# Hybrid decoder block on one core: two of the four mixer sums are split straight from their tiles, and block four splits its key, value and gate weights from the raw matrix

## The chip, the cores and the metric

The kernel runs on one NeuronCore of a Trainium2 chip. Five engines work side by side and meet through semaphores: PE (TensorE, matmuls, with PEld for the weight loads that overlap them), DVE (VectorE), ACT (ScalarE), POOL (GpSimd) and SP (SyncE, which issues most DMAs here). The metric is device time in microseconds (us) of one execution, as a median over several runs.

## The reference, cut to what matters

One layer of a hybrid decoder on 2048 tokens of width 1024, all in float32. The parts that the change touches are the combined projection and what makes its right-hand sides:

```
h = RMSNorm_pre(x) * (1 + scale) + shift
one combined projection h W_in -> [attn q|k|v, mLSTM q|k|v|o, mLSTM i|f pre-gates, branch gates A|B]
branch A: causal sliding-window (128) GQA, rotary on q/k, learned per-head sinks, banded blocks
branch B: causal depthwise conv4 + SiLU on mLSTM q/k, chunkwise-parallel stabilised mLSTM,
          per-head layer norm, sigmoid output gate
merged = sigmoid(g_A) * (y_A W_A) + sigmoid(g_B) * (y_B W_B); mix = merged W_out
x = x + gate * RMSNorm_post(mix); same sandwich + adaLN for the SwiGLU FFN.
```

Attention has 8 query heads and 2 key/value heads of 64; the mLSTM has 4 heads of 128 and chunks of 64. The FFN is 2816 wide.

## The kernel before

**Arithmetic.** Float32 products are made from a rounded high part (`hi`, fp32r) and the remainder (`lo`). mm3 (L212) issues three matmuls for each product: hi by hi, hi by lo, lo by hi. So every operand must first be split: ACT casts it (`A.copy` to fp32r), DVE subtracts the cast from the original. Where an operand is used again, both parts are kept in DRAM ("kept weights") and loaded as pairs, which saves the split.

**Tiling.** The 2048 tokens are four blocks of 512 (b = 0 to 3), called block one to block four here; a superblock sb has two blocks, b0 = 2 sb and b1 = 2 sb + 1. Around the change PE projects, in order, the mLSTM's values for b0 (`vm`), then for b1 key, value and gate pre-activations (`kv`, 264 columns), the query (`q`, 512 columns) and `vm`, with attention and mLSTM steps woven in. A `token_group` takes the weights in pieces of two or four 128-row slabs and accumulates into four PSUM tiles, one for each 128 tokens; when the last piece is done it evacuates the four tiles with ACT (L870 in `vm`, L840 in `kv`), each into a `tx` buffer, from where a DMA stores them. PSUM has four such accumulators, so the next product needs them evacuated.

**The sums.** For the large products after that (the mLSTM's output gate, q and k, and the branch gates, for a whole superblock: `in_pair`) the kernel uses a Strassen-Winograd scheme over the two blocks of a superblock. Its right-hand sides are sums T1 to T4 of h tiles, each 128 x 2048 (1 MB); they stand as plain float32 in tiles of the pool `big` (dictionary HR, written by DVE at L558 to L561). `hsums` splits them into `hi` and `lo` tiles, also of the pool `big`, entered in the dictionary HC by `hc_part(name, i)`. It is called twice for each superblock: for T2 and T4 between `vm` of b0 and `kv` of b1 (L1382), and for T1 and T3 after the rest of `vm` of b1 (L1394). Before, each call copies both sums with a DMA from SBUF to SBUF into the `lo` tile (L569), yields for L_HD (5000), and then makes eight casts (L575) and eight subtractions (L576) of 128 x 512 in place, with a yield of L_HS (1500) after each.

**The weights.** `Raw` tiles hold raw weights (pool `raw`, two buffers), `split` (L267 ACT, L268 DVE) makes the parts (four buffers of each part), `piece` makes the two into a `Part`. For key, value and gates, `load_kv` takes 256 columns of w_in as rows of 1 KB (L819) and 8 columns as rows of 32 bytes (L820). Block one and block two read these raw weights and split them; block two stores the parts in W_D["kv"] (L374, eight stores of 264 KB, because `store` is "kv" when b is not 0). Block three and block four load the parts from there: two loads of 1056 KB each, each into a raw tile (L333), and no split. The query's weights of blocks three and four come as kept parts too: every second piece goes into a raw tile (L333), the others into a pair of split tiles (L328, two loads of 512 KB).

**What sets the order.** Generators yield small steps; a list of pending streams (`spawn`, `tick`, `finish`) is woven with the matmuls by a clock of estimated ns (the L_ numbers), and the Tile scheduler then fixes each engine's list of instructions and its semaphores. Once fixed, each engine works through its own list in order: an ACT cast that waits for a DMA holds up each evacuation behind it, and a DMA on SP's list whose data isn't ready holds up the loads behind it. In these lists every DMA of SP takes one of eight semaphores in turn (DMAHW0 to 7).

**Names in rows.** acc and mix are PSUM tiles; big are the 1 MB tiles of h, of T1 to T4 and their parts; hl is a split pair of `in_pair`'s weights; whi and wlo are parts of weights; at_d, at carry attention operands through DRAM; tm, sp, mx belong to the mixers; vm_d and vmt are the DRAM and SBUF side of `vm`'s result.

Of the kernel before, what the change touches and what calls it, by code (L numbers as in the profile page):

```python
# [10 lines left out]
F32 = mybir.dt.float32  # L11
# [4 lines left out]
ALU = mybir.AluOpType  # L16
# [12 lines left out]
T2 = 1024  # L29
# [9 lines left out]
L_X, L_HT, L_HS = 16000.0, 1400.0, 1500.0  # L39
# [34 lines left out]
def decoder_block(ctx: ExitStack, tc: tile.TileContext, a: dict, out: bass.AP, dbg=None):  # L74
    nc = tc.nc
# [18 lines left out]
    V, A, T, Q = (InOrder(e) for e in (nc.vector, nc.scalar, nc.tensor, nc.sync))  # L94
# [35 lines left out]
    def big(shape, dtype=F32):  # L130
        t = bpool.tile([P, 2048], dtype, tag="big", name=nm("big"))
        return t.rearrange("p (k c) -> p k c", k=shape[0])
# [86 lines left out]
    def spawn(gen, delay=0.0):  # L219
        st = [now[0] + delay, gen, False]  # L220
        streams.append(st)
        return st
# [15 lines left out]
    def finish(sts):  # L238
        for st in sts:
            while not st[2]:  # L240
                now[0] = max(now[0], min(q[0] for q in streams))
                tick()
# [75 lines left out]
    def kept_weights(name):  # L318

        n = 528 if name == "kv" else 1024  # L320
        for j0 in range(0, 4, 2):
            for j in ((j0,) if name == "kv" else (j0, j0 + 1)):
                def load(j=j):
                    src = W_D[name]
                    if name != "kv" and j % 2:
                        parts = [split_tile(x) for x in ("whi", "wlo")]
                        for i in range(2):
                            nc.sync.dma_start(parts[i].bitcast(F32), src[:, j, i, :])  # L328
                        return [parts]
                    m = 2 if name == "kv" else 1  # L330
                    t = wpool.tile([P, RAWC], F32R, tag="raw", name=nm("raw"))
                    v = t[:, :m * 2 * n].rearrange("p (m i c) -> p m i c", m=m, i=2)
                    nc.sync.dma_start(v.bitcast(F32), src[:, j:j + m, :, :])  # L333
                    return [[v[:, q, i, :] for i in range(2)] for q in range(m)]
                raw = Raw(load)
                for q in range(2 if name == "kv" else 1):
                    yield raw, q, 2 * (j + q), 2
# [41 lines left out]
    def srcs_rows(w, nk, c0):  # L379
        for k0 in range(0, nk, 4):  # L380
            kn = min(4, nk - k0)
            raw = raw_rows(w, k0, kn, c0)
            for j in range(0, kn, 2):
                yield raw, (lambda t, j=j: t[:, j:j + 2, :]), k0 + j, 2
# [110 lines left out]
    HC, HR = {}, {}  # L495

    def hc_part(name, i):
        st = HC.setdefault(name, [None, None])
        if st[i] is None:
            st[i] = big([4, TB], F32R)  # L500
        return st[i]
# [59 lines left out]
            V.tensor_tensor(t4, t4, t2, op=ALU.subtract)  # L561
            yield L_HT

    def hsums(names):

        for name in names:
            raw = HR.pop(name)
            lo = hc_part(name, 1)
            nc.sync.dma_start(lo.bitcast(F32), raw)  # L569
        yield L_HD  # L570
        for name in names:
            hi, lo = (hc_part(name, i) for i in range(2))
            for k in range(4):
                v = lo[:, k, :].bitcast(F32)
                A.copy(hi[:, k, :], v)  # L575
                V.tensor_tensor(lo[:, k, :], v, hi[:, k, :].bitcast(F32), op=ALU.subtract)  # L576
                yield L_HS

    def norm_out(xy, t, dst_n, sx):

# [188 lines left out]
    def superblock(sb):  # L769
# [3 lines left out]
        def lhs_h(b):  # L773
            def lhs(kk, t):
                return tuple(p_[:, kk % 4, t * P:(t + 1) * P] for p_ in HC[f"{kk // 4 + 1}{b % 2 + 1}"])
            return lhs
# [33 lines left out]
        def evac_q(b):  # L810
            def evac(t, ps):
                raw = tx([P, 512])
                A.copy(raw, ps)
                R["qk"].append(spawn(q_stream(b, t, rope(raw, HQ, b, t))))
            return evac
# [19 lines left out]
        def evac_kv(b):  # L835
            before = [v_last]

            def evac(t, ps):
                raw = ld([1, 512])[:, 0, :] if b == 0 else tx([P, 392])
                A.copy(raw[:, :264], ps[:, :264])  # L840
                v, dv = raw[:, 128:256], raw[:, 264:392]
                n = b * NT + t
                y = rope(raw, HKV, b, t)
                for i in range(2):
                    A.copy(gt[:, t, 32 * i:32 * i + 4], raw[:, 256 + 4 * i:260 + 4 * i])
                V.tensor_tensor(dv, v, before[0], op=ALU.subtract)
                before[0] = v
                if t == NT - 1:
                    A.copy(v_last, v)
                    before[0] = v_last  # L850
                G.dma_start(at_d[n][:, AT_V + P:], dv)
                if n + 1 < S // P:
                    G.dma_start(at_d[n + 1][:, AT_V:AT_V + P], v)
                R["qk"].append(spawn(k_stream(n, y)))
            return evac

        def q_kv(b):
            if b > 1:
                q = token_group(kept_weights("q"), KD, 512, lhs_h(b), evac_q(b), kept=True)
            else:  # L860
                q = token_group(srcs_rows(w_in, KD, C_Q), KD, 512, lhs_h(b), evac_q(b), pair_heads=True, store="q" if b else None)
            if b > 1:
                return q, token_group(kept_weights("kv"), KD, 264, lhs_h(b), evac_kv(b), kept=True)
            raw_kv = Raw(load_kv)
            return q, token_group([(raw_kv, (lambda r, j=j: r[:, j:j + 2, :]), j, 2) for j in range(0, KD, 2)], KD, 264, lhs_h(b), evac_kv(b), store="kv" if b else None)
# [194 lines left out]
        def attend(b):  # L1060
            finish(R["qk"])
            ready[0] = (b - b0 + 1) * NT
            if b == b0:
                R["att"] = [spawn(attention_stream(0), L_QK), spawn(attention_stream(1), L_QK + L_ATT2)]
            R["gs", b] = [spawn(gates(b), L_QK)]
# [313 lines left out]
        yield lambda: finish([hps[b1]])  # L1379
        if sb == 0:  # L1380
            yield lambda: attend(b0)
        yield lambda: hps.update(t=spawn(hsums(("T2", "T4"))))  # L1382
        q1, kv1 = (list(z) for z in q_kv(b1))
        yield from kv1
        yield from q1
# [5 lines left out]
        def start_f():  # L1391
            finish([hps["t"]])
            HC.pop("12")
            hps["t"] = spawn(hsums(("T1", "T3")))  # L1394

        yield start_f
        pairs = [("om", 0), ("qk", 0), ("om", 1), ("qk", 1), ("ga", 0), ("qk", 2), ("ga", 1), ("qk", 3),
# [22 lines left out]
    hps = {}  # L1420
# [780 lines left out]
    def program():  # L2201
        items = [it for sb in range(NSB) for it in superblock(sb)]
        last = max(i for i, it in enumerate(items) if isinstance(it, Part))
        first_block()
        yield from items[:last]
        yield lambda: next(phase2)
        yield from items[last:]
# [47 lines left out]
```

## Time and profile before

| what | before |
|---|---|
| median of 3 runs | 2662.91 us (2662.21 to 2664.54) |
| profiled execution | 2668.66 us, its span 2667.0 us |
| mean granted clock of PE in it | 0.994 |
| bytes moved by DMA | 532.97 MB, mean 200 GB/s |
| SBUF to SBUF copies of L569 | 8, of 1024 KB each |
| stores of L374 (kv, q, vm parts) | 24 |

One execution is profiled; it is 5.75 us above the median of the runs. The span runs from the first to the last instruction, and 1.66 us of that execution lie around it. In a timeline's row stand the start (us in the span), the duration, the engine, the line, the operation, out<-in, the shape, the count, and in brackets the idle time before it with what ended it. "PEclk" is the share of full clock that PE was granted. A DMA's row on SPq is its issue; "DMA to landing" is the time from there until the data is in place.

### The profile page before, as it was taken

To read this page: it belongs to the slowest core of one execution; us is meant where nothing else is said; L and a number is where in the kernel's file an instruction comes from. 1 tells how busy PE (TensorE), PEld (TensorE's weight loads), DVE (VectorE), ACT (ScalarE), POOL (GpSimd) and SP (SyncE) were. 2 spreads that over 40 slices of the span, in tenths; PEclk is the share of its full clock that TensorE was granted. 3 is DMA by queue.
4 is the path that set the end of the run, shared out by engine and by line. 5 is a ranking of instruction groups with operands and counts; after the bars stand their busy time and mean duration, and the time that the engine had idled before them with its cause. 6 is when DMAs were issued, how large, how long until landed. Compare 5 with 4: busy or idle time off the path is not lost.

```text
span 2667.0 us, 36229 instructions
## 1 busy us (share of the span) xinstructions
PE 2615.5 (98%) x12546; PEld 2145.8 (80%) x12546; DVE 1937.2 (73%) x3758; ACT 1281.9 (48%) x2531; POOL 300.3 (11%) x473
## 2 busy tenths in 40 slices
PE   8999999999989999999999999999999999999998
PEld 6877788888876788888878888888778888888876
DVE  5878887768676988875777777775776767676466
ACT  6656544545654654454643433345554333333444
POOL 0320001101132000210001111110000011001000
PEclk9899999999999999999999999999999999999999
DMA  7785465887787545597765554446675323234556
GB/s 270 255 303 164 135 196 183 291 301 253 262 313 244 166 135 181 183 296 268 220 238 193 184 169 153 163 139 228 213 242 173 111 99 116 90 111 139 199 196 220
DMA packets 327032, 532.97 MB, mean 200 GB/s; under 512 B 23136, under 2 KB 197724, under 8 KB 320064
## 3 DMA queue, kind: packets, MB, share of 16 engines
q1 hardware_dynamic: 287752, 448.45, 50.4%
q0 software_dynamic: 20880, 66.41, 6.6%
q10 hardware_dynamic: 18216, 15.79, 1.9%
q8 instruction: 99, 1.62, 0.2%
q14 instruction: 85, 0.70, 0.1%
HBM read 367.61 MB, written 154.57 MB: 196 GB/s over the span
## 4 chain that ended last, share of the span: by engine, by line
PE 88%; DVE 4%; DMA 3%; ACT 2%; issue 1%; POOL 0%; ACTq 0%; SPq 0%; DVEq 0%; POOLq 0%
PE acc L212 62%; PE mix L212 22%; PE mix L217 2%; PE acc L90 1%; DVE hl L1745 1%; PE mix L90 1%; DMA raw<-as_d 1%; ACT hl L1744 1%; DMA big<-big 0%; DMA raw<-ws_d 0%; DMA raw<-in_w_in_dram 0%; ACT tm L1002 0%; DMA at_d<-tx 0%; DMA raw<-in_w_ffn_down_dram 0%; ACT big L575 0%
## 5 line engine op out<-in xcount | busy, mean ns | idle before, releaser
L212 PE MATMUL acc<-big,hl 128*128 128x512 f32 x3936 | 936.4, 393 | 7.0 <-ACT tx L870 5.4
L212 PEld LDWEIGHTS acc<-big,hl 128*128 128x128 f32 x3936 | 733.8, 188 | 166.4 <-ACT tx L870 5.9
L1744 ACT CAST hl<-raw 128x512 fp32r<-128x512 f32 x732 | 439.9, 621 | 489.6 <-PE acc L212 208.7
L1745 DVE TENSOR_TENSOR hl<-raw,hl 128x512 fp32r<-128x512 f32 x732 | 495.1, 692 | 198.4 <-ACT hl L1744 196.0
L212 PE MATMUL acc<-whi,big 128*128 128x512 f32 (+1 forms) x896 | 281.6, 390 | 3.0 <-ACT tx L870 3.0
L212 PE MATMUL mix<-big,hl 128*128 128x512 f32 x1056 | 263.0, 390 | 1.8 <-ACT hl L1744 1.1
L212 PE MATMUL acc<-hl,hl 128*128 128x512 f32 x1008 | 237.2, 393 | 6.2 <-DVE hl L1745 3.3
L212 PEld LDWEIGHTS mix<-big,hl 128*128 128x128 f32 x1056 | 197.8, 188 | 44.5 <-ACT hl L1744 2.0
L212 PEld LDWEIGHTS acc<-hl,hl 128*128 128x128 f32 x1008 | 187.1, 188 | 51.8 <-DVE hl L1745 8.8
L212 PEld LDWEIGHTS acc<-whi,big 128*128 128x128 f32 x896 | 168.6, 192 | 36.2 <-ACT tx L870 3.4
L212 PE MATMUL mix<-hl,hl 128*128 128x512 f32 x792 | 182.7, 391 | 3.4 <-ACT hl L1744 2.6
L212 PEld LDWEIGHTS mix<-hl,hl 128*128 128x128 f32 x792 | 147.8, 188 | 37.6 <-ACT hl L1744 4.2
L212 PE MATMUL acc<-wlo,big 128*128 128x512 f32 (+1 forms) x448 | 174.4, 389 | 0.0
L212 PE MATMUL acc<-big,whi 128*128 128x512 f32 x512 | 157.3, 393 | 0.0
L268 DVE TENSOR_TENSOR wlo<-raw,whi 128x1024 fp32r<-128x1024 f32 (+1 forms) x76 | 90.8, 1194 | 65.7 <-ACT whi L267 60.2
L267 ACT CAST whi<-raw 128x1024 fp32r<-128x1024 f32 (+1 forms) x76 | 78.4, 1032 | 109.7 <-PE acc L212 103.5
L492 POOL TENSOR_TENSOR rs<-ms,halves 128x1 f32<-128x1 f32 (+1 forms) x56 | 41.3, 744 | 797.8 <-DVE ms L490 750.4
L212 PE MATMUL mix<-hcT4h,hl 128*128 128x512 f32 x352 | 115.6, 389 | 0.7 <-ACT hl L1744 0.7
L212 PE MATMUL acc<-hcT2h,hl 128*128 128x512 f32 x352 | 115.5, 389 | 0.0
L212 PEld LDWEIGHTS acc<-big,whi 128*128 128x128 f32 x512 | 95.3, 188 | 19.3
L212 PEld LDWEIGHTS acc<-wlo,big 128*128 128x128 f32 x448 | 85.8, 192 | 18.0 <-issue 1.2
L212 PE MATMUL acc<-big,wlo 128*128 128x512 f32 x256 | 97.6, 392 | 0.0
(388 smaller groups left out, 3802.3 us busy)
## 6 DMA issues: line engine op xcount, KB each, us to landing
as_d<-w POOLq DMA_DIRECT2D x154, 256.0 KB, 2.5
raw<-in_w_in_dram SPq DMA_DIRECT2D x36, 1024.0 KB, 5.4
raw<-as_d SPq DMA_DIRECT2D x70, 512.0 KB, 3.8
raw<-in_w_ffn_gate_dram SPq DMA_DIRECT2D x22, 1024.0 KB, 6.1
raw<-in_w_ffn_up_dram SPq DMA_DIRECT2D x22, 1024.0 KB, 5.8
raw<-ws_d SPq DMA_DIRECT2D x40, 512.0 KB, 4.6
tx<-in_w_ada_dram SPq DMA_DIRECT2D x64, 256.0 KB, 5.3
g_d<-tx SPq DMA_DIRECT2D x64, 256.0 KB, 2.4
```

What stands on the lines that cost most here:

```text
L90: self.last = tc.keep_in_program_order(f(*p, **k)).ins
L212: T.matmul(o, lhsT=lhsT, rhs=rhs, start=start, stop=stop, skip_group_check=resumed)
L217: T.transpose(o, i, ident[:k, :k])
L267: A.copy(hv, src)
L268: V.tensor_tensor(lv, src, hv.bitcast(F32), op=ALU.subtract)
L492: G.tensor_tensor(r[:, :n], ms[:, :n], nhalf[:, :n], op=ALU.pow)
L1744: A.copy(v(hi), src)
L1745: V.tensor_tensor(v(lo), src, v(hi).bitcast(F32), op=ALU.subtract)
```

## The change

Two edits, and one that follows from the first.

1. `hsums(name, moved)` splits its first sum (T2, then T1) straight from its own tile into new `hi` and `lo` tiles, in four steps with a yield of L_HS after each, with no copy and no wait. Only then the sum's tile is given back, the second sum (T4, then T3) is copied by DMA into its `lo` tile as before, and after L_HD it is split in place as before. Of eight copies four are left.
2. In `q_kv` the kept parts of key, value and gates are read by block three alone (b == 2). Block four goes the way of block two: one raw load of 1 MB and 32 KB from w_in, four splits, and, since `store` is "kv" there too, eight stores of the parts into W_D["kv"], which nobody reads afterwards. The two loads of 1056 KB are gone.

In the changed kernel the lines stand three lower behind hsums (the evacuation of `vm` is L873, the kept loads stay at L333, the store at L374), the direct split is L568 and L569, the copy L573, the split in place L578 and L579, `load_kv` L822 and L823.

```diff
-    def hsums(names):
-
-        for name in names:
-            raw = HR.pop(name)
-            lo = hc_part(name, 1)
-            nc.sync.dma_start(lo.bitcast(F32), raw)
+    def hsums(name, moved):
+
+        hi, lo = (hc_part(name, i) for i in range(2))
+        for k in range(4):
+            A.copy(hi[:, k, :], HR[name][:, k, :])
+            V.tensor_tensor(lo[:, k, :], HR[name][:, k, :], hi[:, k, :].bitcast(F32), op=ALU.subtract)
+            yield L_HS
+        HR.pop(name)
+        lo = hc_part(moved, 1)
+        nc.sync.dma_start(lo.bitcast(F32), HR.pop(moved))
         yield L_HD
-        for name in names:
-            hi, lo = (hc_part(name, i) for i in range(2))
-            for k in range(4):
-                v = lo[:, k, :].bitcast(F32)
-                A.copy(hi[:, k, :], v)
-                V.tensor_tensor(lo[:, k, :], v, hi[:, k, :].bitcast(F32), op=ALU.subtract)
-                yield L_HS
+        hi = hc_part(moved, 0)
+        for k in range(4):
+            v = lo[:, k, :].bitcast(F32)
+            A.copy(hi[:, k, :], v)
+            V.tensor_tensor(lo[:, k, :], v, hi[:, k, :].bitcast(F32), op=ALU.subtract)
+            yield L_HS
...
-            if b > 1:
+            if b == 2:
                 return q, token_group(kept_weights("kv"), KD, 264, lhs_h(b), evac_kv(b), kept=True)
...
-        yield lambda: hps.update(t=spawn(hsums(("T2", "T4"))))
+        yield lambda: hps.update(t=spawn(hsums("T2", "T4")))
...
-            hps["t"] = spawn(hsums(("T1", "T3")))
+            hps["t"] = spawn(hsums("T1", "T3"))
```

How the lists move. First ACT at place 1, T2/T4 of the first superblock, while `vm` of block one ends: whi139 and whi145 are the first two parts of block two's key/value weights, tx141 to tx144 the four evacuations of `vm`, big171 and big206 the high parts of T2 and T4 before. Before:

```order
L267 CAST whi139_1092<-raw121_935 128x528
L575 CAST big171_1252<-big151_1147 128x512 x4
L870 COPY tx141_1104<-acc122_938 128x512
L870 COPY tx142_1113<-acc123_939 128x512
L267 CAST whi145_1134<-raw121_935 128x528
L829 CAST tx114_912<-mix131_989 128x128
L803 ACTIVATE tx126_945<-mix134_1015 128x512
L803 ACTIVATE tx127_950<-mix135_1024 128x512
L575 CAST big206_1495<-big152_1149 128x512 x4
L870 COPY tx143_1122<-acc124_940 128x512
L870 COPY tx144_1131<-acc125_941 128x512
```

and after, with big151 and big200 the high parts of T2 and T4:

```order
L568 CAST big151_1147<-big64_543 128x512
L267 CAST whi139_1092<-raw121_935 128x528
L873 COPY tx141_1104<-acc122_938 128x512
L873 COPY tx142_1113<-acc123_939 128x512
L267 CAST whi145_1134<-raw121_935 128x528
L873 COPY tx143_1122<-acc124_940 128x512
L832 CAST tx114_912<-mix131_989 128x128
L873 COPY tx144_1131<-acc125_941 128x512
L806 ACTIVATE tx126_945<-mix134_1015 128x512
L806 ACTIVATE tx127_950<-mix135_1024 128x512
L578 CAST big200_1448<-big184_1340 128x512 x4
L267 CAST whi159_1195<-raw121_935 128x528
```

T2's casts now lie further up (the last of the four is the first row), all four evacuations stand ahead of T4's casts, and T4's casts ahead of whi159, the third part of the key/value weights.

Next SP at place 3, T2/T4 of the second superblock and block four's key and value. big1323 and big1324 are the lo tiles of T2 and T4, raw1239 and raw1265 the two raw tiles, at1223 an attention operand, vm_d2 the stores of block three's evacuations. Before:

```order
L476 DMA tx1264_7713<-in_w_ada_dram 128x512
L569 DMA big1323_8010<-big1141_6927 128x2048
L954 DMA at1223_7481<-at_d8_198 128x1792
L569 DMA big1324_8012<-big1067_6529 128x2048
L333 DMA raw1239_7547<-w_kv_d_227 128x2112
L476 DMA tx1282_7798<-in_w_ada_dram 128x512
L328 DMA whi1339_8117<-w_q_d_226 128x1024
L328 DMA wlo1340_8118<-w_q_d_226 128x1024
L333 DMA raw1265_7721<-w_kv_d_227 128x2112
L871 DMA vm_d2_212<-tx1297_7888 128x512
L871 DMA vm_d2_212<-tx1298_7897 128x512
```

and after, with big1343 the lo tile of T4:

```order
L476 DMA tx1264_7712<-in_w_ada_dram 128x512
L476 DMA tx1282_7797<-in_w_ada_dram 128x512
L957 DMA at1223_7479<-at_d8_198 128x1792
L822 DMA raw1239_7545<-in_w_in_dram 128x8x256
L823 DMA raw1239_7545<-in_w_in_dram 128x8x8
L874 DMA vm_d2_212<-tx1299_7893 128x512
L573 DMA big1343_8116<-big1067_6527 128x2048
L333 DMA raw1265_7720<-w_q_d_226 128x2048
L874 DMA vm_d2_212<-tx1300_7902 128x512
L957 DMA at1238_7543<-at_d9_199 128x1792
L374 DMA w_kv_d_227<-whi1297_7881 128x528
L476 DMA tx1311_7971<-in_w_ada_dram 128x512
```

T2's copy is gone, the raw load stands ahead of T4's copy, T4's copy has moved behind the store of an evacuation, and raw1265 now takes the query's first piece. Further down on SP, the stores of the last parts and the next two loads of query weights (raw1348, and whi1346 with wlo1347, the second piece) stand like this:

```order
L374 DMA w_kv_d_227<-whi1334_8072 128x528
L374 DMA w_kv_d_227<-wlo1335_8073 128x528
L374 DMA w_kv_d_227<-whi1344_8133 128x528
L374 DMA w_kv_d_227<-wlo1345_8134 128x528
L333 DMA raw1348_8167<-w_q_d_226 128x2048
L328 DMA whi1346_8139<-w_q_d_226 128x1024
L328 DMA wlo1347_8140<-w_q_d_226 128x1024
```

Before, the second query piece (whi1339 and wlo1340 there) stood on SP ahead of the second key/value load, as the piece of the list before shows; now it stands behind the stores of the third and fourth parts.

## The prediction

> **What bounds the kernel now.** I read the page's first table and its chain of work, then PE's waits, the windows around them, and the timelines at each gap.
>
> ```profile
> PE 2615.5 (98%) x12546; PEld 2145.8 (80%) x12546; DVE 1937.2 (73%) x3758; ACT 1281.9 (48%) x2531; POOL 300.3 (11%) x473
> PE 88%; DVE 4%; DMA 3%; ACT 2%; issue 1%; POOL 0%; ACTq 0%; SPq 0%; DVEq 0%; POOLq 0%
> ```
>
> PE is busy for 2615.5 of 2667.0 us and makes 88% of the chain. Only 51.5 us are idle, and work taken from ACT, DVE or the DMA engines shortens the kernel only where PE stands still for it, or runs slowly because it stood still. The change touches hsums, which runs four times (T2/T4 and T1/T3 in each superblock), and the key/value weights of block four, which fall beside the third of these. So there are four places. PE's waits there, between 85 and 200 us, then between 740 and 870 us:
>
> ```profile
> PE acc L212 <- ACT tx L870: 3.8, 3, 2.7
> PE mix L217 <- DVE tm L1035: 1.2, 1, 1.2
> PE mix L217 <- DVE tm L912: 0.3, 1, 0.3
> ...
> PE acc L212 <- ACT tx L870: 4.6, 1, 4.6
> PE acc L212 <- ACT tm L985: 4.2, 1, 4.2
> PE mix L217 <- DVE tm L987: 2.6, 1, 2.6
> ```
>
> These are 16.7 us (columns: total, times, longest). Beside them stands the clock. The windows give PE's busy time first, and after the engines the granted clock, the DMA share and GB/s:
>
> ```profile
> 105.00:110.00 5.00, 2.31 (x14) 2.10 (x14) 3.55 (x7) 1.66 (x5) 1.43 (x3) 0.78 0.88 336
> 110.00:115.00 5.00, 4.73 (x28) 4.33 (x28) 4.91 (x11) 1.29 (x3) 1.49 (x3) 0.50 0.98 293
> 115.00:120.00 5.00, 5.00 (x27) 4.78 (x26) 3.19 (x12) 3.47 (x10) 0.00 (x0) 0.50 1.05 377
> 120.00:125.00 5.00, 5.00 (x33) 4.45 (x32) 2.99 (x16) 4.07 (x18) 2.08 (x2) 0.85 0.29 107
> 750.00:785.00 35.00, 28.18 (x201) 25.27 (x201) 26.42 (x83) 17.63 (x55) 10.85 (x17) 0.95 1.02 381
> 845.00:858.00 13.00, 9.17 (x53) 7.31 (x51) 7.47 (x17) 1.55 (x3) 2.59 (x5) 1.00 0.99 359
> 858.00:866.00 8.00, 7.28 (x26) 5.64 (x26) 8.00 (x16) 5.93 (x13) 0.00 (x0) 0.79 1.03 404
> ```
>
> Busy time at a clock below 1.00 is partly lost: busy times (1 - clock). These two rows, both of 128x512 matmuls, the first in the stretch at 0.79, bear that out:
>
> ```profile
> 858.72 7.34 PE L212 MATMUL acc<-big,hl 128*128 128x512 f32 x24 [4.55 <-ACT tx L870]
> ...
> 785.55 4.36 PE L212 MATMUL acc<-raw,big 128*128 128x512 f32 x18
> ```
>
> 7.34 / 24 = 0.306 us against 4.36 / 18 = 0.242: a ratio of 0.79.
>
> **The change, part by part.** First what it takes from and gives to the engines.
>
> ```profile
> L575 ACT CAST big<-big x32: 602/616/648, 93.3 to 869.9; 128x512 fp32r<-128x512 f32 x32
> ...
> DMA to landing us min/median/max: 4.4/6.3/15.5
> ...
> L267 ACT CAST whi<-raw x76: 632/1055/1096, 61.6 to 1358.7; 128x1024 fp32r<-128x1024 f32 x72, 128x528 fp32r<-128x528 f32 x4
> L268 DVE TENSOR_TENSOR wlo<-raw,whi x76: 685/1224/1227, 63.9 to 1359.8; 128x1024 fp32r<-128x1024 f32 x72, 128x528 fp32r<-128x528 f32 x4
> ```
>
> The 32 casts and 32 subtractions of hsums stay; four of its eight 1 MB copies (the landing row is theirs) go.  Block four adds four casts and four subtractions of 128x528, at the least times of those rows: 4 x 0.63 = 2.5 us of ACT and 4 x 0.69 = 2.7 us of DVE. ACT is 48% busy and DVE 73%, so I cost them at nothing as long as the weights land before PE needs them; uncovered, one piece costs 0.63 + 0.69 = 1.3 us. The useless stores (8 x 264 KB = 2.16 MB) and the raw load (1.08 MB) stand against a removed copy (1.05 MB) and two removed loads of 1.08 MB: in 750 to 785 us the bytes stay as they were, and only their order changes.
>
> *Place 1, T2/T4 of the first superblock.* ACT's timeline, then PE's, then SP's:
>
> ```profile
> 102.09 2.18 ACT L575 CAST big<-big 128x512 fp32r<-128x512 f32 x4 [2.05 <-DMA big<-big]
> 108.34 0.59 ACT L870 COPY tx<-acc 128x512 f32<-128x512 f32 x1 [3.58 <-issue]
> ...
> 104.80 0.39 PE L212 MATMUL acc<-whi,big 128*128 128x264 f32 x1 [0.31 <-ACT tx L870]
> 108.97 0.59 PE L212 MATMUL acc<-whi,big 128*128 128x264 f32 x1 [2.69 <-ACT tx L870]
> ...
> 91.83 0.63 SPq L569 DMA_DIRECT2D big<-big  x1
> ...
> 95.96 1.31 SPq L871 DMA_DIRECT2D vm_d<-tx  x2
> ```
>
> ACT stands 2.05 us for T4's copy, which took from 91.83 to about 102.1, and casts for 2.18 with two finished accumulators behind it; the last of these also waits for a tx buffer whose store POOL issued late (3.58). PE gets that bank 2.69 us late and falls to half clock. Idle, with the 0.3 for DVE from the waits: 0.31 + 2.69 + 0.3 = 3.3. Clock: 2.31 x 0.22 + 4.73 x 0.5 + 5.0 x 0.5 + 5.0 x 0.15 = 6.1. In the changed order all four accumulators are evacuated ahead of T4's casts, and the last one's tx buffer hangs on the store of the first evacuation instead, issued near 96 us; with the median landing of 6.3 it is free near 102, where PE asked for the bank at 108.97 - 2.69 = 106.28. T4's copy goes behind that store on SP, near 97 instead of 91.8. It lands near 103 by the median, near 107 by the 10.3 us of its predecessor, and its casts stand in ACT's queue ahead of the third key/value piece; PE has two pieces to work on first, 48 matmuls of 264 columns (0.242 x 264 / 512 = 0.125 us each, 6 us), so until about 111: cover enough at 107, not beyond. Bounds 0 and 3.3 + 6.1 = 9.4 gained. I take -6, nearer the far end, since every wait of the old chain is gone, and leave 3.4 for a shorter one behind T4's casts.
>
> [...]
>
> *Place 2, T1/T3 of the first superblock.*
>
> ```profile
> 187.38 0.66 PE L217 MATMUL mix<-ident,tx 128*128 128x128 f32 x4 [1.22 <-DVE tm L1035]
> 192.50 4.83 PE L212 MATMUL acc<-big,hl 128*128 128x512 f32 x20 [0.82 <-ACT tx L870]
> ```
>
> 2.0 us are idle at full clock. T1's casts need no copy now, but T3's copy goes behind a weight load and its casts stand in ACT's queue at the same mixing work. Bounds -2 and +2, taken 0.
>
> *Place 3, T2/T4 of the second superblock and block four's key and value.*
>
> ```profile
> raw<-w_kv_d SPq DMA_DIRECT2D x2, 1056.0 KB, 14.9
> ...
> 752.22 1.46 SPq L333 DMA_DIRECT2D raw<-w_kv_d  x1
> ...
> 757.72 2.47 SPq L871 DMA_DIRECT2D vm_d<-tx  x2
> ...
> 751.04 12.34 DMA big<-big
> ...
> 763.41 2.18 ACT L575 CAST big<-big 128x512 fp32r<-128x512 f32 x4 [5.22 <-DMA big<-big]
> ...
> 760.21 1.80 PE L212 MATMUL mix<-at 64*128 64x256 f32 x24
> 766.18 3.07 PE L212 MATMUL acc<-raw,big 128*128 128x264 f32 x14 [4.18 <-ACT tm L985]
> ...
> 784.73 1.06 PE L217 MATMUL mix<-ident,tm 128*128 128x128 f32 x8 [2.64 <-DVE tm L987]
> ```
>
> The wait's name is a copy of ACT's, but what ends last is the kept weights: issued at 752.22 behind T2's copy, an attention load and T4's copy, 13 to 16 us to landing (median of the two loads 14.9), so about 766. Idle 4.18; slow clock 28.18 x 0.05 = 1.4; and 2.64 later for the scores' chain. Now the raw load stands ahead of both the T4 copy and the stores, behind one attention load alone. The same 1 MB transfer for block two, in a quieter time, landed so:
>
> ```profile
> DMA to landing us min/median/max: 5.4/5.4/5.4
> ```
>
> Its raw buffer comes free where the kept load's did, at 752.2, so it lands near 758 (the 32 KB of gate weights ride behind it); cast and subtraction of the first piece end near 762, when PE has done its 1.80 us. What is late next is T4: its copy waits on SP behind a store of an evacuation (757.72), lands 6.3 to 8 us later, 764 to 766, and its four casts stand in ACT's queue ahead of the last evacuation. PE wants its fourth bank after 18 matmuls of 0.125, near 764.2, and gets it after four casts (2.2) and the evacuation (0.5): it stands 2.5 to 4.5 us. I take 3, a gain of 4.18 + 1.4 - 3 = 2.6, and leave 2.64 where it is. A second trap is the query's second weight piece: its load is now behind the stores of the fourth key/value piece, which wait for that piece's subtraction. Cover: the first query piece, 24 matmuls at 0.242 = 5.8 us. I charge +1. Net -1.6, rounded to -2, bounds -5.6 and +8 (rival 3).
>
> [...]
>
> *Place 4, T1/T3 of the second superblock.*
>
> ```profile
> 845.62 11.34 DMA raw<-in_w_in_dram
> ...
> 857.05 1.14 ACT L1744 CAST hl<-raw 128x512 fp32r<-128x512 f32 x2 [8.55 <-DMA raw<-in_w_in_dram]
> ```
>
> PE waits 4.55 us for a weight load that shares a full DMA (0.99) with both copies, and then loses 7.28 x 0.21 = 1.5 to the clock. One copy is gone and the other is issued after the next weight load: 1.05 MB at 359 GB/s is 2.9 us less ahead of the load. Bounds 0 and -6; taken -3.
>
> Sum: -6 + 0 - 2 - 3 = -11. The profiled run took 2668.66 (span 2667.0 and 1.66 around it), so the profiled run after would be near 2657.7. The median of before is 2662.91, 5.75 under its profiled run; with the same sum the median after is 2652. A measurement of this kernel can tell about 0.2%, 5.3 us, from no change.
>
> **The rivals.**
>
> 1. *The clock does not pay* (14%). If PE still has some short wait at each place, the half clock returns and only idle goes: 3.3 - 0.5 at place 1, 2 at place 3, 2 at place 4, less the 1: about -5.8, or 2657.1, on the bound of 0.2%. [...] For it: 2.69 us idle was enough for 10 us at half clock. Against: at place 1 no wait of the old chain is left.
>
> 2. *Other work takes the place of the waits* (16%). The DMA share stays 1.02 and 0.99 at places 3 and 4 and no byte is saved at the first of these; PE then waits for T4's casts or the query weights instead, and place 1 alone gives, half of its 6: 2660, within 0.2%. [...] For it: the bytes. Against: the load that PE waits for now stands first.
>
> 3. *Slower: T4's and T3's copies land late with ACT's queue behind them* (13%). In place 3 the copy, issued near 757.5, lands after 12.34 us as it did before, near 770; four casts (2.2) and the evacuation (0.5) end near 772.6, PE has stood since 764.2: 8.4 idle and some 5 of slow clock as at place 1, against 5.6 before: +8. The same lateness takes place 4's gain, adds 2 at place 2, and leaves half of place 1's gain: +8 + 2 - 3 = +7, or 2670. At place 3 it decides from a landing 8.2 us after issue: 765.7 + 2.7 - 764.2 = 4.2, what PE stood before. For: the copies' maximum of 15.5. Against: their median of 6.3, and that two loads fewer are ahead.
>
> That the change doesn't do what it says is excluded by the order: block four has its raw load, its casts and its stores, and four of the eight copies are gone.
>
> **How the numbers follow.** The forecast, -11, has 57%. Faster by over 0.2% (under 2657.6) is it and half of rival 1: 0.64. Same is the other half and rival 2: 0.23. Slower is rival 3: 0.13. The low end has places 1, 3 and 4 at their best, -9.4 - 5.6 - 6 = -21: 2642. The high end goes past rival 2 to 2664 and leaves out rival 3 and little else.
>
> **What would show it.** Right: PE's wait of 2.69 for an evacuation and the clock of 0.50 at 110 to 120 are gone; block four's first key/value matmul starts within 3 us of the end of the mixing before it; PE's 4.55 near 858 has shrunk to 2 or less. Wrong in part: a PE wait for an evacuation behind casts of L578 (rival 3), a wait for query weights after 775 (my +1 too small), or the same idle under a new releaser with the DMA share still at 1.0 (rival 2).

## The result, and the profile after

| | before | after |
|---|---|---|
| median of 20 runs each | 2662.86 us (2660.16 to 2666.00) | 2666.62 us (2662.94 to 2670.25) |
| ratio | | 1.0014, 95% interval 1.0008 to 1.0021 |
| profiled execution | 2668.66 us, clock 0.994 | 2662.97 us, clock 0.996 |

The kernel became 3.8 us slower; -11 was forecast. Single slow runs of 3745 us in e6 and of 8276 us in e10, below, are left out of their medians. The two profiled executions say the opposite: after is 5.7 us faster than before. The one of before lies above all 20 of its timed runs, the one of after near the lower end of its own. So the two pages, held against each other, lead astray by some 9 us, and the first question is what in a single profile is the kernel and what is that execution.

The first table of the page after:

```profile
PE 2617.2 (98%) x12546; PEld 2143.4 (81%) x12546; DVE 1943.8 (73%) x3762; ACT 1283.3 (48%) x2535; POOL 299.4 (11%) x473
```

PE is idle for 2661.2 - 2617.2 = 44.0 us instead of 51.5, so waits did go, but it is busy for 1.7 us more. PE's waits after, first from 85 to 200 us, then from 735 to 870:

```profile
PE mix L217 <- POOL tm L1008: 2.2, 1, 2.2
PE acc L212 <- DVE wlo L268: 1.9, 2, 1.1
PE acc L212 <- ACT tx L873: 0.8, 1, 0.8
PE mix L212 <- ACT tm L1017: 0.3, 1, 0.3
...
PE acc L212 <- ACT tx L873: 2.4, 1, 2.4
PE acc L212 <- ACT whi L267: 2.4, 1, 2.4
PE mix L212 <- ACT tm L1017: 1.9, 2, 1.8
PE acc L212 <- DVE wlo L268: 0.7, 1, 0.7
```

In the first superblock the wait of 2.7 for an evacuation is gone, and 5.2 us of others stand there (5.3 before). In the second, 4.6 at place 4 and 4.2 at place 3 have become 2.4 each, with 0.7 more for a second weight piece at place 3; the 2.6 of the scores' chain is gone, and the 1.9 stood at 1.7 before. The windows around place 1 after (PE's busy time first, then after the engines clock, DMA share, GB/s):

```profile
105.00:110.00 5.00, 3.86 (x39) 3.23 (x38) 4.97 (x9) 1.06 (x4) 2.19 (x5) 1.00 1.02 379
110.00:115.00 5.00, 4.37 (x43) 4.10 (x41) 4.28 (x12) 2.00 (x6) 0.00 (x0) 1.00 1.06 391
115.00:120.00 5.00, 4.12 (x28) 3.60 (x28) 4.01 (x22) 3.89 (x14) 1.08 (x2) 1.00 0.96 319
120.00:125.00 5.00, 3.53 (x14) 3.04 (x15) 4.35 (x15) 5.00 (x20) 3.37 (x4) 0.66 0.50 201
```

The half clock is down from 0.22 + 0.5 + 0.5 + 0.15 of 5 us each, that is 6.85 us of lost clock time or 13.7 us at half clock, to 0.34 x 5 = 1.7, or 3.4 us. That one difference, 5.1 us, is most of the 5.7 between the profiles.

What keeps PE waiting there now, on PE, then ACT, then DVE:

```profile
109.33 0.39 PE L212 MATMUL acc<-wlo,big 128*128 128x264 f32 x1 [1.14 <-DVE wlo L268]
115.17 0.39 PE L212 MATMUL acc<-wlo,big 128*128 128x264 f32 x1 [0.80 <-DVE wlo L268]
121.47 1.11 PE L217 MATMUL mix<-ident,tm 128*128 128x128 f32 x4 [2.18 <-POOL tm L1008]
...
102.50 2.18 ACT L578 CAST big<-big 128x512 fp32r<-128x512 f32 x4 [0.93 <-DMA big<-big]
109.80 0.64 ACT L267 CAST whi<-raw 128x528 fp32r<-128x528 f32 x1 [2.61 <-DMA w_kv_d<-whi]
...
107.41 1.26 DVE L579 TENSOR_TENSOR big<-big,big 128x512 fp32r<-128x512 f32 x2
108.59 0.69 DVE L268 TENSOR_TENSOR wlo<-raw,whi 128x528 fp32r<-128x528 f32 x1
```

T4's subtractions stand on DVE ahead of the third key/value part, which PE then waits for; the fourth part's cast waits for a store to free its buffer. The evacuations are through, and the splits behind them are the next thing late.

At places 3 and 4 the loads come earlier and PE waits less, as the prediction had it, though not by as much as it had. The chain's rows for the two loads that PE waits for, PE's rows behind them, and the windows with the clock:

```profile
752.04 9.89 DMA raw<-in_w_in_dram
...
762.70 0.78 PE L212 MATMUL acc<-whi,big 128*128 128x264 f32 x2 [2.38 <-ACT whi L267]
...
844.53 8.88 DMA raw<-in_w_in_dram
...
855.11 2.07 PE L212 MATMUL acc<-big,hl 128*128 128x512 f32 x4 [2.44 <-ACT tx L873]
...
760.00:765.00 5.00, 2.62 (x12) 1.96 (x10) 3.72 (x9) 1.99 (x5) 0.52 (x1) 0.78 1.05 404
765.00:770.00 5.00, 5.00 (x25) 5.00 (x25) 4.91 (x12) 3.42 (x7) 0.00 (x0) 0.54 1.00 367
855.00:860.00 5.00, 4.89 (x22) 3.70 (x23) 4.91 (x13) 2.92 (x9) 0.00 (x0) 0.67 1.06 408
```

The raw load lands at 761.9, where 758 was forecast and the kept one landed near 766; the load at place 4 takes 8.88 instead of 11.34 us. But the slow clock did not shrink with the idle time: (0.22 + 0.46) x 5 = 3.4 us lost on the clock at place 3, 6.8 us at half clock against 3.4 before, and at place 4 the same 3.4 us at half clock as before.

### The profile page after: what moved, and what is told of

It is laid out like the page before. It is cut to its first block, busy times and chain, and to the rows that moved or that the text cites. A ratio compares the mean times of both kernels' runs of the same rounds, so it can differ in the third digit from the quotient of the medians.

```text
span 2661.2 us, 36228 instructions
## 1 busy us (share of the span) xinstructions
PE 2617.2 (98%) x12546; PEld 2143.4 (81%) x12546; DVE 1943.8 (73%) x3762; ACT 1283.3 (48%) x2535; POOL 299.4 (11%) x473
## 4 chain that ended last, share of the span: by engine, by line
PE 88%; DVE 5%; DMA 3%; ACT 2%; issue 1%; POOL 0%; ACTq 0%; SPq 0%; DVEq 0%; POOLq 0%
PE acc L212 62%; PE mix L212 22%; PE mix L217 2%; DVE hl L1748 1%; PE acc L90 1%; PE mix L90 1%; DMA raw<-in_w_in_dram 1%; ACT hl L1747 1%; DMA raw<-as_d 1%; ACT tm L1005 1%; DMA raw<-ws_d 0%; DMA big<-in_x_dram 0%; DVE big L1748 0%; DMA raw<-in_w_ffn_down_dram 0%; DVE big L579 0%
## 5 line engine op out<-in xcount | busy, mean ns | idle before, releaser
L212 PE MATMUL acc<-whi,big 128*128 128x512 f32 (+1 forms) x960 | 293.4, 382 | 2.4 <-ACT whi L267 2.4
L212 PEld LDWEIGHTS acc<-whi,big 128*128 128x128 f32 x960 | 178.4, 190 | 36.7 <-ACT whi L267 2.6
L212 PE MATMUL acc<-wlo,big 128*128 128x512 f32 (+1 forms) x480 | 182.9, 382 | 2.7 <-DVE wlo L268 2.7
L212 PEld LDWEIGHTS acc<-wlo,big 128*128 128x128 f32 x480 | 91.4, 190 | 20.4 <-DVE wlo L268 3.6
```

The source lines that it names most:

```text
L212: T.matmul(o, lhsT=lhsT, rhs=rhs, start=start, stop=stop, skip_group_check=resumed)
```

## The experiments

The first theory (A) was that the first profile's slow clock at place 1 is not in the median, and that beyond it the first superblock loses. The rival (B) put the loss on block four's split and its stores. Where runs of the kernel before are named, they ran on the same chip beside the experiment (15 to 29 of them); a mean clock is that of all runs of a kernel.

**e1, the sums' edit alone.** In the changed kernel:

```diff
-            if b == 2:
+            if b > 1:
                 return q, token_group(kept_weights("kv"), KD, 264, lhs_h(b), evac_kv(b), kept=True)
```

> The first edit alone: T2 and T1 are split straight from their tiles, block four still loads its kept key/value parts. Theory A (the profiled run of before held about 5 us of slow clock at place 1 that the median doesn't hold; beyond that the first superblock loses about 3.5 us at equal clock and place 4 wins about 2.5): about 2663 to 2665, within 0.1% of before. Theory B (the key/value split of block four with its stores costs what the sums win): 2658 or less, 0.2% under before.

Measured: 2673.72 (5 runs), ratio 1.0044 (1.0032 to 1.0057). Both theories missed: the sums' edit alone costs 12 us, and block four's split gives back 8 of it.

**e2, block four's edit alone.** The kernel before, with the same line the other way round (`b > 1` to `b == 2`).

> The second edit alone: the sums as before, block four splits its key/value weights and stores the parts. Theory A: about 2661, 1 to 2 us under before, since the weights that PE waited for until 766 land earlier. Theory B: 2667 or more, the whole loss of the change or more.

Measured: 2661.97, ratio 1.0003 (0.9994 to 1.0012): no difference that can be told. B falls, and the gain that A had doesn't show either. Mean clock and time move apart: 0.9946 against 0.9959 of before. Mean time by mean clock, about what the run would take at full clock, is 2648.3 against 2650.3, and the slow clock (mean time by 1 - clock) costs 14.3 us against 11.0: some 2 us of other time are won, and the slow clock takes them back. They are not won where the prediction had it. PE's waits in e2's profile from 735 to 870 us are these:

```profile
PE acc L212 <- ACT whi L267: 5.2, 1, 5.2
PE acc L212 <- ACT tx L870: 3.3, 2, 2.8
PE acc L212 <- DVE wlo L268: 1.3, 1, 1.3
```

With the sums as before the raw load stands on SP behind both copies, and the stall at block four's weights is 5.2 and 1.3 us, longer than the 4.2 of before. What goes is the wait of 2.6 for the scores and part of the one at place 4. So the shorter stall of the changed kernel comes with the sums' edit and not with the raw load: in e1's profile, where T2's copy is gone too and the kept parts are loaded ahead of T4's copy, PE waits 0.7 us there.

**e3, no useless stores.**

```diff
-... lhs_h(b), evac_kv(b), store="kv" if b else None)
+... lhs_h(b), evac_kv(b), store="kv" if b == 1 else None)
```

> The changed kernel without the eight useless stores of block four's parts (2.16 MB). Theory A: as the changed kernel, 2666 to 2667. Theory B: 3 us or more under it, 2663, if the stores hold up SP and the buffers of the parts (the cast of the third part waited for a store's landing for 3.9 us in the changed kernel's profile).

Measured: 2667.73, ratio 1.0026 (1.0016 to 1.0035). The 2.16 MB of stores cost nothing that is seen. B falls a second time.

**e4, the kernel before again**, no edit.

> The kernel before, unchanged, for a second profile and for what two equal kernels differ by. Theory A: ratio 1.000 within 0.0006, and in the profile a half clock of 3.4 or 6.8 us near 110 us, where the first profile had 13.7; Theory B needs nothing of it, and the half clock of 13.7 us stands there again if it belongs to the stall itself.

Measured: 2661.91, ratio 1.0004 (0.9995 to 1.0012). The windows of this second profile at place 1:

```profile
105.00:110.00 5.00, 3.35 (x26) 2.92 (x24) 4.99 (x12) 2.22 (x6) 2.90 (x5) 1.00 1.02 392
110.00:115.00 5.00, 3.33 (x33) 3.15 (x34) 4.86 (x12) 2.49 (x5) 0.00 (x0) 1.00 1.04 378
115.00:120.00 5.00, 5.00 (x39) 4.55 (x38) 3.20 (x21) 4.99 (x22) 1.56 (x2) 1.00 0.94 338
120.00:125.00 5.00, 5.00 (x29) 4.33 (x28) 5.00 (x21) 4.88 (x23) 4.28 (x8) 1.00 0.78 295
```

PE's two waits there:

```profile
107.15 0.39 PE L212 MATMUL acc<-whi,big 128*128 128x264 f32 x1 [1.24 <-ACT tx L870]
111.67 0.44 PE L217 MATMUL mix<-ident,tm 68*128 68x68 f32 x4 [2.08 <-DVE tm L912]
```

PE is idle for 3.3 us here as in the first profile, though in two pieces of 1.24 and 2.08 us where the first had one of 2.69 and two of 0.3; and the clock is 1.00 throughout, where A had 3.4 or 6.8 us of half clock. The same code had 13.7 us of half clock in one execution and none in another. Over the eight profiles with the first superblock's sums as before (before, e2, e4, e9, e10, e12, e13, e15) it was 13.7, 3.4, 0, 3.4, 3.4, 0, 0 and 6.8 us between 86 and 198 us, 3.8 in the mean, which is 1.9 us lost. Over the five with T2 and T4 as in the changed kernel (after, e1, e3, e6, e11) it was 3.4, 6.8, 6.8, 3.4 and 3.4 us, 4.8 in the mean.

With e4 as the measure, the loss of the changed kernel could be placed. Two marks that stand in every profile bound a stretch of the first superblock: the first product of `in_pair` after place 2 (PE, with 0.82 idle before it), and a copy of ACT near 330 us. In e4:

```profile
187.09 12.78 PE L212 MATMUL acc<-big,hl 128*128 128x512 f32 x55 [0.82 <-ACT tx L870]
...
328.52 0.58 ACT L1214 COPY tx<-acc 128x512 f32<-128x512 f32 x1 [1.51 <-PE acc L212]
```

and after, the same two:

```profile
189.18 12.56 PE L212 MATMUL acc<-big,hl 128*128 128x512 f32 x54 [0.82 <-ACT tx L873]
...
332.64 0.59 ACT L1217 COPY tx<-acc 128x512 f32<-128x512 f32 x1 [1.50 <-PE acc L212]
```

141.43 us against 143.46, with PE idle for less than 0.1 us and the clock at 1.00 in both. Busy PE, same matmuls, 2.0 us more. What differs is their order. Theory C: PE alternates more often between the projection and the matmuls of attention, and each change costs. Rival D: T4's late copy, with its casts in ACT's queue, is the loss.

**e5, T1 alone split straight.** The changed kernel, with the old function kept beside the new as hsums_copied:

```diff
-        yield lambda: hps.update(t=spawn(hsums("T2", "T4")))
+        yield lambda: hps.update(t=spawn(hsums_copied(("T2", "T4"))))
```

> The changed kernel with T2 and T4 copied and split as before; only T1 is split straight, and block four splits its key/value weights. PE's list of instructions changes product (line or PSUM tag) 135 times in the first 15% of the matmuls, against 124 before and 147 in the changed kernel. Theory C (the sums' edit shifts the weave in the first superblock: some 23 more changes between projection and mixing matmuls at about 0.13 us each, 3 us, with PE never idle): about 1.5 us of loss in the first superblock, the gain of 2 to 3 at place 4 kept, so 2661 to 2663. Theory D (T4's late copy with its casts in ACT's queue is the loss): no loss at place 1, 2659 to 2660.

Measured: 2667.09, ratio 1.0016 (1.0008 to 1.0025), mean clock 0.9945: slower than either theory said; by mean clocks all of it is slow clock (14.8 us against 10.8), though single profiles put 2.0 us into the stretch between the marks. D falls, since T4's copy is the old one here. The stretch takes 143.47.

**e6, T2 alone split straight**: the same for the other call.

```diff
-            hps["t"] = spawn(hsums("T1", "T3"))
+            hps["t"] = spawn(hsums_copied(("T1", "T3")))
```

> The changed kernel with T1 and T3 copied and split as before; only T2 is split straight, and block four splits its key/value weights. 148 changes of product in the first 15% of PE's list. Theory C: the whole loss of the first superblock (3 us at equal clock) and no gain at place 4: 2668 to 2670. Theory D: the same loss, but as idle time of PE between 100 and 130 us; the matmuls after 200 us then run as in the kernel before.

Measured: 2675.26 (5 runs), ratio 1.0048 (1.0035 to 1.0061), more than C had. The stretch takes 143.42, so either call by itself gives the order that costs 2.0 us there. Against e4, its profile loses 1.2 us more ahead of the first mark, 6.6 in the second superblock up to 868 us, and 3.6 at the start of the FFN (below). Why the second superblock loses so much without T1's straight split was not followed up.

**e7, the copy first.**

```diff
     def hsums(name, moved):
+        lo = hc_part(moved, 1)
+        nc.sync.dma_start(lo.bitcast(F32), HR.pop(moved))
+        yield L_HD
...
-        lo = hc_part(moved, 1)
-        nc.sync.dma_start(lo.bitcast(F32), HR.pop(moved))
-        yield L_HD
-        hi = hc_part(moved, 0)
+        hi, lo = (hc_part(moved, i) for i in range(2))
```

> The changed kernel with the order inside hsums as before: first the copy of T4 (T3), then the yield of L_HD, then T2 (T1) split straight, then T4 (T3) in place. 130 changes of product in the first 15% of PE's list. Theory C: under 1 us of loss in the first superblock, the matmuls between 200 and 330 us as before; about 2661, no slower than before. Theory D: T4's copy is early again and its casts behind T2's as before, so the stall of place 1 (1.2 and 2.1 us in the second profile of before) comes back and nothing else: also about 2661; they part in e5 and e6.

Measured: 2672.45 (5 runs), ratio 1.0034 (1.0022 to 1.0046): a miss for both. The stretch takes 142.48, in between, as C has it, but the mean clock is 0.9932, 18.2 us lost against 10.8, and the stall at place 1 is back (1.64 and 2.23 us in its profile).

**e9, e10, e11: the change by superblocks.** e9 has the whole change where sb is 1 and the old calls where it is 0; e10 the same with T2/T4 old everywhere; e11 the new sums where sb is 0 and nothing else. Theory E is C's rival here.

```diff
-        yield lambda: hps.update(t=spawn(hsums("T2", "T4")))
+        yield lambda: hps.update(t=spawn(hsums("T2", "T4") if sb else hsums_copied(("T2", "T4"))))
...
-            hps["t"] = spawn(hsums("T1", "T3"))
+            hps["t"] = spawn(hsums("T1", "T3") if sb else hsums_copied(("T1", "T3")))
```

> The whole change in the second superblock alone: the first superblock's four sums are copied and split as before, so PE's list there has the 124 changes of product of the kernel before. Theory C (the loss is the finer alternation of projection and mixing matmuls in the first superblock): the changed kernel less about 3 us, 2663, and perhaps 1 to 2 under before, since the idle time at places 3 and 4 falls by about 4 and slow clock takes part of it back. Theory E (the loss is made in the second superblock, by new waits and slow clock there): as the changed kernel or slower, 2666 or more.

> In the second superblock T1 alone is split straight and block four splits its key/value weights; T2 and T4, and the whole first superblock, are as before. Theory C: the loss of about 2 us that the run with T1/T3 alone showed between 197 and 330 us is gone, so 2662 to 2664 against its 2667. Theory E: 2666 to 2667.

> The sums' edit in the first superblock alone; the second superblock and block four as before. 147 changes of product in the first 15% of PE's list. Theory C: 3 to 4 us slower than before, 2665, with no more idle time of PE before 335 us than before; the later stages run as in the kernel before. Theory E: as before, 2662.

Measured: e9 2666.38, ratio 1.0019 (1.0010 to 1.0027); e10 2666.98, 1.0015 (1.0006 to 1.0024); e11 2666.29, 1.0016 (1.0007 to 1.0024). e11 is as C said: the first superblock's sums alone cost 4.4 us against 2661.90 beside it, and the later stages run as before. e9 and e10 are as E said. By mean clocks all of e10's loss is slow clock (16.2 us against 11.5), and almost none of e9's (12.1). So the change loses in the second superblock as well, though PE's idle time between 745 and 879 us falls by 3.2 in e9's profile against e4. The losses do not add up: either superblock alone costs as much as both; no run shows why.

**e12 and e13: the order alone, without the change.** In the kernel before, one constant of the weave each:

```diff
-L_SOFT, L_PT, L_PV = 8000.0, 1300.0, 1000.0
+L_SOFT, L_PT, L_PV = 8000.0, 2000.0, 1000.0
```

```diff
-L_ML, L_KW, L_OUT, L_STATE = 3200.0, 2600.0, 1500.0, 1500.0
+L_ML, L_KW, L_OUT, L_STATE = 3200.0, 2600.0, 2500.0, 1500.0
```

> The kernel before, none of the change in it, with one weave constant of attention (L_PT, 1300) set to 2000. Its list of PE has 135 changes of product in the first 15% of the matmuls (9 more of them in the stage from 198 to 330 us) and 7 more beside block four. Theory C (each change between projection and mixing matmuls costs PE 0.1 to 0.2 us without being idle): the stage from 198 to 330 us is 1.0 to 1.7 us longer with no idle time and no slow clock in it; the whole 2663 to 2666. Rival (the 2.0 us there come with the sums' tiles or copies, not with the alternation): that stage takes the time of before within 0.3 us.

> The kernel before with another weave constant (L_OUT, 1500) set to 2500: 14 changes of product fewer in the fifth part of PE's list from 15% to 20%, 3 more in the next. Theory C: the stage from 330 to 745 us is 1.5 to 2 us shorter, at no idle time before and after; the whole 2660, 0.05 to 0.1% under before. Rival: no difference in that stage.

Measured: e12 2660.58, ratio 0.9997 (0.9988 to 1.0006); e13 2661.92, 1.0000 (0.9991 to 1.0009). The two marks in e12:

```profile
185.47 2.79 PE L212 MATMUL acc<-big,hl 128*128 128x512 f32 x11 [0.87 <-ACT tx L870]
...
328.41 0.59 ACT L1214 COPY tx<-acc 128x512 f32<-128x512 f32 x1 [1.51 <-PE acc L212]
```

142.94 us: 1.5 more than in e4 without any part of the change, 0.2 of it idle, as C said. The whole, 2663 to 2666 by C, was a miss: by mean clocks e12 takes 1.4 us more at full clock, but its slow clock was 8.7 us against 10.9. e13 had 11 changes of product fewer between 330 and 745 us and gained nothing there (0.0 us against e4), where C had 1.5 to 2. So e13's changes of product show no cost, 0.0 us for 11 of them: they are between matmuls that all fill 128 x 128. What costs here is a change of shape, to attention's 64 x 128 and 128 x 64 matmuls and back. Counted so, between the two marks:

| changes of shape | kernels | time between the marks, us |
|---|---|---|
| 24 | before, e2, e4, e9, e10, e13 | 141.1 to 141.8 |
| 28 | e14 | 142.0 |
| 30 | e7 | 142.5 |
| 32 | e12 | 142.9 |
| 34 | after, e1, e3, e5, e6, e11 | 143.4 to 143.5 |

That is 0.2 us for each (e15, with 28, has 144.5, of which 2.05 are idle). The rows show the form. Timeline of PE after, then in e4, at the same part of attention:

```profile
230.11 1.52 PE L212 MATMUL mix<-tm,at 128*64 128x256 f32 x12
231.56 0.73 PE L212 MATMUL acc<-big,hl 128*128 128x512 f32 x2
232.22 1.08 PE L212 MATMUL mix<-tm,at 128*64 128x256 f32 x8
233.24 2.56 PE L212 MATMUL acc<-big,hl 128*128 128x512 f32 x10
235.73 0.65 PE L212 MATMUL mix<-tm,at 128*64 128x256 f32 x4
236.31 0.96 PE L212 MATMUL acc<-big,hl 128*128 128x512 f32 x3
```

```profile
229.91 1.51 PE L212 MATMUL mix<-tm,at 128*64 128x256 f32 x12
231.35 1.89 PE L212 MATMUL acc<-big,hl 128*128 128x512 f32 x7
233.17 2.38 PE L212 MATMUL mix<-tm,at 128*64 128x256 f32 x20
235.48 0.73 PE L212 MATMUL acc<-big,hl 128*128 128x512 f32 x2
```

The narrow matmuls come in runs of 12, 8 and 4 after, where e4 has 12 and 20. From start to start a run of 20 takes 2.31 us, of 8 1.02, of 4 0.58: 0.11 for each matmul and 0.15 for the run. The full ones between them do likewise: runs of 2, 7 and 10 take 0.66, 1.82 and 2.49 us, 0.23 for each and 0.2 for the run. One more run of each kind is two more changes and costs about 0.35, near what the table has. All these changes go to attention's matmuls and back, so the shape isn't told apart from what else is special to those.

**e14 and e15: the order put back inside the changed kernel.** Theory F is C in this form. L_PV from 1000 to 1500, in the changed kernel and, as a control, in the kernel before.

> The changed kernel with one weave constant of attention (L_PV, 1000) set to 1500, which takes its list of PE from 130 changes between attention's narrow matmuls and full 128 x 128 ones back to 116, the number of the kernel before; in the first superblock 48 instead of 60. Theory F (the measured loss of the first superblock is these changes of shape, 0.1 to 0.2 us each): 12 fewer there make 1.5 to 2 us, so about 2664 to 2665 against 2666.6, and the stages from 86 to 330 us take what they take before but for slow clock. Rival (other parts of the sums' edit cost it): 2666 to 2667 as without the constant.

> The kernel before with the same constant set to 1500: 124 changes of shape against 116, 8 more. Theory F: about 1 us slower than before, 2663, within what can be told; the stage from 86 to 330 us about 0.5 to 1 longer at the same idle time and clock. Rival: the constant by itself makes a gain of 1.5 us or more, and then what the changed kernel wins by it says nothing of the sums' edit.

Measured: e14 2672.26 (5 runs), ratio 1.0037 (1.0023 to 1.0050); e15 2662.16, 1.0001 (0.9992 to 1.0010). The control lost 1.0 us of busy time between the marks, as F said, and 2.0 of idle time there, which F did not have; as a whole it is no slower. e14 has its stretch back to 141.96, 1.5 under the changed kernel, as F said. The whole is a miss: between 86 and 198 us it has 4.2 us more idle time than e4 and 5.0 more lost on the clock. No experiment beat both kernels; e12 is nearest, and can't be told from before.

One more loss turned up in e1, e6 and e14, far from the edit, at the start of the FFN. PE's wait there in e1 and in e14, which e4 and the changed kernel don't have (e6 has 1.9):

```profile
PE acc L212 <- ACT w L1888: 1.8, 1, 1.8
```

```profile
PE acc L212 <- ACT w L1888: 3.7, 1, 3.7
```

With the slow clock behind it, e1, e6 and e14 lose 2.2, 3.6 and 5.2 us against e4 there.

## Why the prediction was wrong, step by step

**The failing step was place 1's -6, and in it the clock.** "Clock: ... = 6.1" was worked out rightly from the rows, but it belongs to that execution. The text noted that the median lies 5.75 us under the profiled run and then took the whole sum from the median all the same: "with the same sum the median after is 2652". 6.1 us of slow clock in a run that is 5.75 over its median was the hint. e4 shows the same code without it, and in the mean of eight profiles 1.9 us stood there to be won, not 6.1. As far as means tell, the slow clock is 11.0 us a run before (26 runs beside e1) and 12.4 after.

**Its idle time was replaced, not removed.** The chain that the prediction followed (T4's cast, evacuation, tx buffer) did go, and T4's copy landed before 102.5, about as forecast. The part "T4's casts stand ahead of the third key/value piece; cover enough" failed by 1.14 us on DVE, and 0.80 and 2.18 followed: 5.2 us in this superblock against 5.3.

**Missing from the sum: what the new order does to PE while it is busy.** PE's list was looked at for its waits only. Between the marks 10 more changes of shape cost 2.0 us; between 86 and 198 us there are 4 more (47 against 43 in e4), and 0.7 more busy time at full clock. Rival 2 ("other work takes the place of the waits") came nearest, but its waits are not what made the kernel slower. Nor did the prediction's signs catch it: in the profile after, the wait of 2.69 and the clock of 0.50 at place 1 are gone, and block four's first key/value matmul comes 2.38 us behind the mixing; only the 4.55 at place 4 has shrunk to 2.44 and not to 2. All of these look at waits and clock, none at PE's busy time.

**Places 2, 3 and 4.** Place 2: 2.0 became 1.2, 0 was forecast. Place 3: 4.18 became 2.38 + 0.72, for half of the reason given: the load stands in front because T2's copy is gone, and the raw load by itself is the slower one (with both copies 5.2 in e2 against 4.2 before with the kept parts, without T2's copy 2.38 against 0.7 in e1). PE waits for the cast of that load rather than for the fourth bank; the 2.64 of the scores, left in place by the forecast, went with block four's split (gone in e2, still 2.5 in e1); the query weights, charged with +1, made no wait. Against that stands twice the half clock of before, in one profile each. Place 4: 4.55 became 2.44 and the load 2.5 us shorter, where -3 and 2.9 were forecast. From 745 to 879 us the profiles of after and e4 differ by -0.9 in all: -3.7 idle, +1.6 clock, +1.2 of busy time at full clock that I did not resolve.

**Rivals.** Rival 1 said that only idle time would go; here the slow clock even grew at place 3, and in e2, by mean clocks, it took 3.3 us against 2 won. Rival 3 did not happen: T4's and T3's copies landed in 6.4 to 7.5 us.

**The account.** After against e4, both from profiles: +2.1 up to the first mark (clock 1.5, busy 0.7, idle -0.1), +2.0 between the marks, -0.9 from 745 to 879, +0.3 for the rest: +3.5. The medians differ by 3.8. That the changes between attention's matmuls and full ones make the +2.0 is shown by e12 and by the table; how much the slow clock adds on average in each stage is not, with one profile for each kernel. Why the second superblock alone (e9) loses 4.5 us stays open: its profile has 3.2 less idle, 2.9 more lost on the clock and 3.4 more busy time than e4 from 745 to 879 us, and 8 more changes of shape explain about half of the last.

## What to carry to other kernels

Before a term of one profile is subtracted from a median, ask whether it belongs to the kernel: a profiled run well above its median holds something that most runs don't, and slow clock after a short stall is the first candidate (here 13.7 us of half clock beside a stall of 2.69). A second profile of the same kernel costs one run; here it would have taken 6 us out of the forecast.

Where a scheduler orders the lists, an edit off the critical path can reorder the engine that sets the time; so count on that engine not only waits but changes between matmul shapes (0.2 us each here). An edit that removes copies and waits can lose to the order that it brings, and then the order is the thing to work on.

## What the runs showed of the hardware

- Going from full 128 x 128 matmuls to attention's 64 x 128 or 128 x 64 ones and back cost PE 0.2 us for each change, in no view an idle gap (141.4 us with 24 changes in e4, 143.5 with 34 after). Changes between products of full shape cost nothing that can be seen (11 fewer in e13, 0.0 us between 330 and 745).
- In the profiles of before and after the half clock came in stretches of 3.4, 6.8 and 13.7 us (the last stretch of each, which its end cuts off, aside). Near 110 us it stood beside stalls of 1 to 3 us, and in nearly the same stall one execution had it (1.03 and 2.12 us idle in e9, 3.4 us of half clock) and another not (1.24 and 2.08 in e4, none). The longest idle piece there goes with it: the eleven profiles where it was 1.72 to 2.19 us had 0 to 6.8 us of half clock, the five where it was 2.23 to 2.97 (e7, e1, before, e5, e15) had 6.8 to 13.7.
- Equal kernels spread over 6 us from run to run (2660.2 to 2666.0). A stretch of 3.4 us at half clock loses 1.7 us (0.34 x 5 between 120 and 125 us after), and the longer runs are those of lower mean clock (a correlation of -0.5 to -0.8 over the runs of before beside each set of experiments), so a few such stretches, by my estimate from the two, make part of the spread. e4's ratio of 1.0004 (0.9995 to 1.0012) is what an experiment here can tell.
